# A two-layer backbone on one core: other places, queues and order around the FFN stage

## The chip, the cores and the metric

The kernel runs on one core of one Trainium2 chip. The metric is the device time of one execution in microseconds (us); the kernel before took 3029.22 us, the median of three runs. PE is TensorE, DVE VectorE, ACT ScalarE, POOL GpSimd. SP is the engine that only issues transfers here. PE, DVE, ACT, POOL and SP each run their own list of instructions in order, and a list is written ahead of time by a planner that goes by its own estimates of durations.

## The reference

Two layers of one trunk, float32 throughout, for 1024 latent tokens and 256 context tokens of width 1024:

```python
for l in range(DEPTH):                       # DEPTH = 2
    need_ctx = l < DEPTH - 1                 # the context leaves after layer 0's keys, values and FFN
    mod_l = split(silu(c) @ mod_w[l] + mod_b[l], 6); mod_c = the same of c_ctx
    h_lat, h_ctx = modulate(rmsnorm(x_lat), ...), modulate(rmsnorm(x_ctx), ...)
    y_lat, y_ctx = hybrid_mixer(h_lat, h_ctx, ...)      # GLA, gMLP and windowed attention, one w_in, one w_out
    x_lat = x_lat + mod_l[2] * rmsnorm(y_lat)
    f_lat = swiglu(modulate(rmsnorm(x_lat), mod_l[3], mod_l[4]), w_gu[l], w_down[l])
    x_lat = x_lat + mod_l[5] * rmsnorm(f_lat)
    if need_ctx: the same two steps for x_ctx with mod_c
def swiglu(h, w_gu, w_down):
    g, u = split(h @ w_gu, 2)                # D_FF = 2816: 22 chunks of 128
    return (silu(g) * u) @ w_down
```

## The kernel before

**Products.** Each float32 product is made of three products of high and low parts (`mm3`, L307). `halve` makes the parts: a cast on ACT (L1404) and a difference on DVE (L1405).

**Layer.** `layer` (L1170) runs projection; GLA (`gla_stream`) and windowed attention (`swa_stream`) merged; `mix_out`; the up stage (`Up.stream`); in layer 0 alone `up_context`; and `down_stage`. Each stage has pools of SBUF, opened and closed on the left or right side, and a pool may lie over one that has closed. The planner orders by whole pools; the waits that it then sets are by tile.

**mix_out (L1250).** The concatenated row tiles `cat` come back from DRAM (`xt`, L1274), are turned on PE (L1269), and meet w_out (L1289), whose rows are loaded by `weight` (L1261) through two staging tiles rg and ru that belong to the up stage. `ao` (GLA, L955) and `co` (attention, L1077) are stored to `cat` by SP, the last `co` of a layer by POOL. `post` and `norm` of a tile give the FFN's input; parts of it (s3, s4, a22) go through DRAM and come back by two buffers `hc` in `waiting` (L1386).

**Up stage.** For each of 22 chunks, seven half-size products of 12 matmuls of 512 columns stand for eight. In order: X = b11·a11, copy p1 (L201, ACT); Y = b21·a12, add g0 (L204, DVE) and its Silu (ACT); X += t2·s2, copy u2 (L211, ACT); Z = t1·s1, copy p5 (L214, ACT); X += t3·s3, add c22 (L223, DVE); Z += b22·s4, add c12 (L230, DVE); X += t4·a22, Silu. Differences of weights for the next chunk are on POOL (L174), results go to DRAM `gd` from POOL.

**Context pass (L1408).** The context's 256 tokens, 22 chunks of 48 matmuls; ch and cl are the halves of its input, loaded by two `hc` (L1427), gh, gl, uh, ul those of the weights.

**Down stage (L1445).** Token halves of five tiles (layer 1: four), each in groups of chunks (`sizes`); a group holds its weights (`weight`, ws, L1456) and activations (`acts`, g), does its products (L1111) and adds into ya (L1118); the last group's tiles go through `post`.

**Background modulation.** While layer 0 runs its FFN, DVE computes seven vectors of modulation that come later: `mod_stream("dve")`, seven pieces of 16 steps, each step a load of 256 KB (ms, L421) and two multiply-adds (macc, L503 and L505); a fold on PE (L447) and transposes (L455) end a piece. `paced` advances it by a step each time the planned costs that the stage yields sum to MOD_STEP = 6.6.

## Time and profile before

| | before |
|---|---|
| median of 3 runs | 3029.22 us (3026.78 to 3031.38) |
| profiled execution | 3032.15 us, span 3030.4 us |
| PE busy | 2802.9 us (92%) |
| DVE busy | 1905.1 us (63%) |
| ACT busy | 1333.0 us (44%) |
| POOL busy | 691.8 us (23%) |
| read and written, over the span | 121 GB/s |

The page gives shares over the whole span, and a share is an average over stages with different limits. So it is read for the engine that carries the chain, and then the trace is asked stage by stage: busy times in a table by stretches, the waits of an engine with what ended them, and the timeline of an engine for one border. Layer 0's w_out begins near 617 us, its up stage near 765, the context pass near 1246, the down stage near 1397; layer 1's w_out near 2190, its up stage near 2318 and its down stage near 2769.

### The profile page before, as it was taken

The page shows a single profiled execution, that of the slowest core. Times are in us where ns is not written, and L with a number is a line of the kernel's source. Part 1 is how long each engine was busy: PE and PEld are TensorE (multiplying, and loading weights), DVE is VectorE, ACT ScalarE, POOL GpSimd, SP SyncE. Part 2 cuts the span into 40 slices and gives each one's busy share as a digit, 9 for nine tenths or more (in the row PEclk, how much of TensorE's full clock was granted, in tenths as well). Part 3 has the DMA queues.
Part 4 walks back from the last instruction along what each step waited for, and adds up shares of the span by engine and source line. Part 5 has one row for each costly group of instructions (what it writes and reads, how often), then busy time and mean ns, then how long its engine had stood idle before and what let it go on. Part 6 is the DMA issues. An engine that isn't in the chain of part 4 may idle for free.

```text
span 3030.4 us, 43735 instructions
## 1 busy us (share of the span) xinstructions
PE 2802.9 (92%) x16296; PEld 2383.9 (79%) x16296; DVE 1905.1 (63%) x3663; ACT 1333.0 (44%) x2739; POOL 691.8 (23%) x562
## 2 busy tenths in 40 slices
PE   6999899989799999897999999999896999999998
PEld 4999788867677778796788899888775788887886
DVE  3565577866947874377578665788757434344576
ACT  4453576745433233343233245477545333334331
POOL 0000233301454445100000000043302455552000
PEclk8999799999899999998999999999998999999999
DMA  7843000055533442586365354200254222224452
GB/s 233 254 141 89 24 12 9 31 199 180 181 96 106 140 131 83 163 253 211 109 208 163 97 148 117 70 8 11 69 190 153 79 77 81 84 81 168 154 195 90
DMA packets 337809, 370.45 MB, mean 122 GB/s; under 512 B 45296, under 2 KB 259068, under 8 KB 337596
## 3 DMA queue, kind: packets, MB, share of 16 engines
q1 hardware_dynamic: 327244, 335.93, 36.0%
q0 software_dynamic: 9632, 29.11, 2.6%
q8 instruction: 128, 2.10, 0.3%
q10 hardware_dynamic: 720, 2.62, 0.2%
q14 instruction: 85, 0.70, 0.1%
HBM read 300.19 MB, written 67.40 MB: 121 GB/s over the span
## 4 chain that ended last, share of the span: by engine, by line
PE 67%; DVE 13%; DMA 9%; ACT 5%; issue 4%; POOL 1%; SPq 1%; DVEq 0%; ACTq 0%; POOLq 0%
PE b L307 35%; PE b L1111 17%; DMA ms<-in_mod_w 3%; PE b L1012 2%; PE b L1030 2%; PE b L1047 2%; DVE macc L505 2%; PE b L1289 2%; PE b L896 1%; DMA ru<-in_w_out 1%; PE b L884 1%; DMA ws<-in_ffn_w_down 1%; ACT hc L1333 1%; DVE pe L1017 1%; DVE z L1311 1%
## 5 line engine op out<-in xcount | busy, mean ns | idle before, releaser
L1111 PE MATMUL b<-dh,g 128*128 128x512 f32 x828 | 229.5, 396 | 22.1 <-ACT dh L1404 18.6
L1111 PE MATMUL b<-wh,g 128*128 128x512 f32 x756 | 210.3, 396 | 1.7 <-DVE ya L1118 1.7
L1111 PEld LDWEIGHTS b<-dh,g 128*128 128x128 f32 x828 | 157.5, 191 | 57.4 <-ACT dh L1404 19.0
L1118 DVE TENSOR_TENSOR ya<-ya,b 128x512 f32<-128x512 f32 x198 | 127.6, 683 | 109.0 <-PE b L1111 108.9
L505 DVE SCALAR_TENSOR_TENSOR macc<-ms,csil,macc 128x512 f32<-128x512 f32 x196 | 171.0, 907 | 32.7 <-DMA ms<-in_mod_w 31.4
L307 PE MATMUL b<-wh,hh 128*128 128x256 f32 (+1 forms) x592 | 173.2, 294 | 8.6 <-DVE hh L540 3.8
L307 PE MATMUL b<-wh,hl 128*128 128x256 f32 (+1 forms) x592 | 171.4, 290 | 1.2 <-DVE hl L541 1.2
L307 PE MATMUL b<-wl,hh 128*128 128x256 f32 (+1 forms) x592 | 171.8, 290 | 0.4 <-DVE wl L614 0.3
L1111 PEld LDWEIGHTS b<-wh,g 128*128 128x128 f32 x756 | 141.8, 188 | 36.2 <-DVE ya L1118 2.2
L614 DVE TENSOR_TENSOR wl<-ws,wh 128x1024 fp32r<-128x1024 f32 (+2 forms) x68 | 79.7, 1177 | 130.1 <-ACT wh L613 130.0
L307 PE MATMUL b<-hh,wh 128*128 128x320 f32 (+1 forms) x472 | 148.8, 315 | 0.0
L307 PE MATMUL b<-hl,wh 128*128 128x320 f32 (+1 forms) x472 | 147.2, 312 | 0.0
L307 PE MATMUL b<-hh,wl 128*128 128x320 f32 (+1 forms) x472 | 146.9, 311 | 0.0
L1111 PE MATMUL b<-dl,g 128*128 128x512 f32 x414 | 130.0, 395 | 0.1
L1036 DVE TENSOR_TENSOR ptl<-b,pth 128x640 fp32r<-128x640 f32 (+2 forms) x144 | 107.5, 746 | 33.9 <-ACT pth L1035 32.6
L613 ACT CAST wh<-ws 128x1024 fp32r<-128x1024 f32 (+2 forms) x68 | 68.8, 1014 | 136.0 <-PE b L307 80.3
L1035 ACT CAST pth<-b 128x640 fp32r<-128x640 f32 (+2 forms) x144 | 91.0, 632 | 75.6 <-PE b L1030 74.6
L307 PEld LDWEIGHTS b<-wh,hh 128*128 128x128 f32 x592 | 114.4, 193 | 12.5 <-issue 5.5
L231 POOL TENSOR_TENSOR ct<-ct,ct 128x512 f32<-128x512 f32 x44 | 71.8, 1631 | 212.8 <-DVE ct L230 184.5
L1111 PE MATMUL b<-wl,g 128*128 128x512 f32 x378 | 119.0, 395 | 0.0
L1017 DVE CUSTOM_DVE_ANT_0 pe<-b,swm,sink 128x640 f32<-128x640 f32 (+1 forms) x128 | 108.1, 845 | 13.8 <-PE b L1012 13.1
L307 PEld LDWEIGHTS b<-wh,hl 128*128 128x128 f32 x592 | 114.4, 193 | 1.6 <-DVE hl L541 1.6
(380 smaller groups left out, 8544.2 us busy)
## 6 DMA issues: line engine op xcount, KB each, us to landing
ws<-in_ffn_w_down SPq DMA_DIRECT2D x88, 512.0 KB, 3.6
ms<-in_mod_w SPq DMA_DIRECT2D x144, 256.0 KB, 3.5
rg<-in_ffn_w_gu SPq DMA_DIRECT2D x66, 512.0 KB, 3.8
ru<-in_ffn_w_gu SPq DMA_DIRECT2D x66, 512.0 KB, 3.9
ws<-in_w_in SPq DMA_DIRECT2D x56, 512.0 KB, 4.4
gd<-ct POOLq DMA_DIRECT2D x88, 256.0 KB, 2.9
gr<-gd SPq DMA_DIRECT2D x44, 320.0 KB, 3.6
gr<-gd SPq DMA_DIRECT2D x44, 256.0 KB, 3.6
```

What stands on the lines that cost most here:

```text
L231: nc.gpsimd.tensor_mul(g0, g0, c12)
L307: mm = lambda x, y, **kw: self.nc.tensor.matmul(out, x, y, skip_group_check=more, **kw)
L505: nc.vector.scalar_tensor_tensor(x, st, c, x, op0=ALU.mult, op1=ALU.add)
L613: nc.scalar.copy(h[:, : kk * nn], st[:, : kk * nn])
L614: nc.vector.tensor_sub(lo[:, : kk * nn], st[:, : kk * nn], h[:, : kk * nn].bitcast(F32))
L1012: nc.tensor.matmul(ps[:, at : at + n * P], b["qs"][:, h, :], kk[:, j * P : (j + n) * P], start=(n_ == 0), stop=(n_ == 1))
L1017: nc.vector.tensor_tensor_reduce(out=p, in0=sc, in1=b["mask"], scale=1.0, scalar=sink, op0=ALU.add, op1=ALU.min, accum_out=mn)
L1030: nc.tensor.transpose(pt[:, j * P : (j + 1) * P], p[:, j * P : (j + 1) * P], self.ident)
L1035: nc.scalar.copy(hi, pv)
L1036: nc.vector.tensor_sub(lo, pv, hi.bitcast(F32))
L1111: nc.tensor.matmul(ps[n], x[:, s], y[:, n * 512 : (n + 1) * 512], start=(c == 0 and pi == 0), stop=(c == nk - 1 and pi == 2))
L1118: nc.vector.tensor_add(y, y, ps[n])
```

## The change

Six things change. (1) rg and ru get a pool of their own (rp, right side), w_out's halves and GLA's tiles are laid out in another order, and all stores of `ao` and `co` go by POOL. (2) `Up.stream` does the first two products of chunks 0 and 1 ahead of everything else, each chunk is cut into `head` and `tail`, and the Silu of g0 stands behind the copies u2 and p5. (3) In layer 0 the last tile's `post` and `norm` come behind these heads; in layer 1 its `post` has a higher priority; the last tile's transposes use one double bank. (4) The modulation starts behind chunk 1, has a step of 5.4 in the up stage and 6.6 in the down stage, none in the context pass; a gate's transposes are put off to a later step. (5) The context pass takes the place of the up stage's first operands (fa), and loads hc ahead of its weights. (6) The down stage lies on the right, its first weights in wp, its activations where the context pass had its input; the second half has six groups instead of seven.

```diff
+        self.head(0)
+        self.prepare(1, "b11")
+        self.prepare(1, "b21")
+        self.head(1)
+        yield 0.0
         for c in range(NFC):
-            yield from self.chunk(c)
+            if c > 1:
+                self.head(c)
+                yield 5.4
+            yield from self.tail(c)
...
         nc.scalar.copy(p5, Z)
-        if more:
+        net.act(g0, g0, AF.Silu)
+        if 1 < n < NFC:
             self.prepare(n, "b11")
             self.prepare(n, "b21")
+        if more:
             self.diff(n, "t1")
...
             if gate:
-                to_rows(ps)
+                self.later = lambda: to_rows(self.b1())
...
-            nc.sync.dma_start(self.cat[i][:, 0:256], ao)
+            nc.gpsimd.dma_start(self.cat[i][:, 0:256], ao)
...
-            (nc.gpsimd if i == blocks[-1] else nc.sync).dma_start(self.cat[i][:, 512:1024], co)
+            nc.gpsimd.dma_start(self.cat[i][:, 512:1024], co)
...
-            self.paced(st)
-            up.close()
+            with tp("rp", "right") as rp:
+                up = Up(self, l, fa, rp, A)
...
+                    next(st)
+                    if need_ctx:
+                        next(rest)
+                        for _ in range(8):
+                            next(st)
+                    for _ in rest:
+                        pass
...
+                self.paced(st, 5.4)
+                up.close()
         if need_ctx:
-            with tp("cu", "right") as cu:
-                self.paced(self.up_context(l, cu, up))
+            with tp("cu", "left") as cu:
+                self.up_context(l, cu, up)
         self.open_hp()
-        with tp("dn", "left") as dn:
-            self.paced(self.down_stage(l, dn, need_ctx, up.gd))
+        with tp("dn", "right") as dn:
+            self.paced(self.down_stage(l, dn, need_ctx, up.gd), 6.6)
...
-        W = [(self.t(wo, f"oh{k}", [P, D], F32R), self.t(wo, f"ol{k}", [P, D], F32R)) for k in range(KC)]
+        W = {}
+        for k in (7, 6, 0, 1, 2, 3, 4, 5):
+            if k == 0:
+                for x in ("ch", "cl"):
+                    self.t(wo, x, [P, KC, P], F32R, bufs=2)
+            W[k] = self.t(wo, f"oh{k}", [P, D], F32R), self.t(wo, f"ol{k}", [P, D], F32R)
...
+        up.load(1)
         waiting(slice(0, 256))
         if need_ctx:
             waiting(slice(256, 512))
+            yield
+            post(order[-1])
+            yield
+            norm(order[-1])
+            return
         yield
-        post(order[-1])
-        if not need_ctx:
-            waiting(slice(256, 384))
+        with self.tc.high_priority(offset=250):
+            post(order[-1])
+        waiting(slice(256, 384))
         norm(order[-1])
...
-            pool, tags = ((dn, ("dl", "dh")), (self.wp, ("wl", "wh")))[loads[0] % 2]
+            pool, tags = ((self.wp, ("wl", "wh")), (dn, ("dl", "dh")))[loads[0] % 2]
...
-        sizes = [[2, 4, 4, 4, 4, 4], [4, 3, 3, 3, 3, 3, 3]]
+        n = len(halves[0]) * P
+        self.t(dn, "g", [P, 2, n], F32R, bufs=8), self.t(dn, "gr", [P, n], bufs=2)
+        sizes = [[2, 4, 4, 4, 4, 4], [4, 4, 4, 4, 4, 2]]
```

## Rows read from the trace of the kernel before

**Rows 1.** The page's part 4: the chain that ended last, share by engine.

```profile
PE 67%; DVE 13%; DMA 9%; ACT 5%; issue 4%; POOL 1%; SPq 1%; DVEq 0%; ACTq 0%; POOLq 0%
```

**Rows 2.** Stages: stretch, length, PE PEld DVE ACT POOL busy (x count), clock, DMA.

```profile
880.00:940.00 60.00, 60.00 (x269) 48.76 (x268) 25.52 (x37) 21.50 (x37) 30.37 (x25) 1.00 0.27 84
940.00:1040.00 100.00, 87.97 (x350) 69.08 (x349) 95.65 (x114) 27.82 (x50) 40.23 (x33) 0.93 0.50 145
1257.00:1397.00 140.00, 132.57 (x1065) 131.26 (x1065) 98.90 (x128) 55.81 (x74) 10.96 (x21) 0.96 0.86 248
2374.00:2769.00 395.00, 395.00 (x1716) 322.70 (x1714) 153.80 (x200) 137.53 (x238) 198.29 (x159) 1.00 0.25 79
```

**Rows 3.** Waits of PE, 813 to 1246 us: awaited: total us, times, longest.

```profile
PE b L307 <- ACT ct L211: 22.1, 8, 3.6
```

**Rows 4.** Timeline of PE at layer 0's w_out: start, us, instruction, idle before.

```profile
626.12 1.22 PE L1289 MATMUL b<-oh,ch 128*128 128x512 f32 x2 [8.99 <-ACT ch L1279]
```

**Rows 5.** Waits of PE, 755 to 840 us.

```profile
PE b L1269 <- DVE ht L1315: 9.5, 1, 9.5
PE b L307 <- ACT ct L211: 5.8, 2, 3.6
```

**Rows 6.** Timeline of PE, layer 1's end of mix_out.

```profile
2336.13 1.94 PE L1269 MATMUL b<-ident,ht 128*128 128x128 f32 x8 [11.81 <-DVE ht L1315]
```

**Rows 7.** Waits of PE, 1257 to 1397 us, the context pass.

```profile
PE b L307 <- ACT ch L1404: 10.9, 1, 10.9
PE b L455 <- DVE gate L465: 4.7, 1, 4.7
```

**Rows 8.** Waits: PE, 1397 to 1760 us; SP, 1390 to 1415 us.

```profile
PE b L1111 <- ACT dh L1404: 18.6, 2, 15.4
SPq L421 <- DVE macc L505: 13.2, 8, 2.6
```

**Rows 9.** Timeline of SP ahead of layer 0's w_out.

```profile
613.40 0.87 SPq L951 DMA_DIRECT2D gld<-gsp  x2
616.60 0.32 SPq L955 DMA_DIRECT2D cat<-ao  x1
616.97 0.42 SPq L1261 DMA_DIRECT2D rg<-in_w_out  x1
```

**Rows 10.** Busy time by stage, the end of layer 0's attention.

```profile
545.00:617.00 72.00, 66.81 (x574) 58.67 (x572) 67.06 (x189) 50.06 (x135) 32.43 (x36) 0.98 0.19 61
```

**Rows 11.** Timeline of POOL, the last store of co in layer 0.

```profile
620.29 0.61 POOL L1077 DMA_DIRECT2D cat<-co  x1 [2.56 <-DVE co L1075]
```

**Rows 12.** The page's part 6: transfer, queue, count, KB each, median us to landing.

```profile
gd<-ct POOLq DMA_DIRECT2D x88, 256.0 KB, 2.9
cat<-co SPq DMA_DIRECT2D x16, 256.0 KB, 2.0
```

**Rows 13.** Busy time of the instructions on macc, 940 to 1040 us.

```profile
940.00:1040.00 100.00, 67.40 (x70) 0.93 0.50 145
```

**Rows 14.** Timelines of PE and DVE: the wait for L211 and the add L223.

```profile
980.49 0.50 PE L307 MATMUL b<-s3h,t3h 128*128 128x512 f32 x1 [2.83 <-ACT ct L211]
987.22 0.68 DVE L223 TENSOR_TENSOR ct<-b,ct 128x512 f32<-128x512 f32 x1
```

**Rows 15.** Timeline of SP ahead of the context pass.

```profile
1248.47 4.60 SPq L1427 DMA_DIRECT2D hc<-hd  x2
```

**Rows 16.** The page's part 5: a cast and a difference of 128 by 1024.

```profile
L614 DVE TENSOR_TENSOR wl<-ws,wh 128x1024 fp32r<-128x1024 f32 (+2 forms) x68 | 79.7, 1177 | 130.1 <-ACT wh L613 130.0
L613 ACT CAST wh<-ws 128x1024 fp32r<-128x1024 f32 (+2 forms) x68 | 68.8, 1014 | 136.0 <-PE b L307 80.3
```

**Rows 17.** Timeline of SP ahead of the down stage.

```profile
1406.88 0.90 SPq L1456 DMA_DIRECT2D ws<-in_ffn_w_down  x2
```

**Rows 18.** Busy time by stage, the kernel's end.

```profile
3004.80:3030.40 25.60, 12.44 (x55) 9.95 (x54) 21.39 (x64) 4.61 (x8) 0.00 (x0) 0.85 0.36 124
```

**Rows 19.** Waits of SP, 2130 to 2240 us.

```profile
SPq L1077 <- DVE co L1075: 47.8, 2, 27.0
```

More of the change, by code (lines that the diff above doesn't have):

```diff
@@ L29 @@
 GLA_SHARE = (105.0, 83.0)
-MOD_SHARE_PROJ, MOD_STEP = 100.0, 6.6
+MOD_SHARE_PROJ = 100.0
 MOD_LATE = 3
@@ L189, in stream, with head @@
     def stream(self):
-        for c in range(NFC):
-            yield from self.chunk(c)
-    def chunk(self, c):
-        nc, net, n = self.nc, self.net, c + 1
-        more = n < NFC
-        X, Y, Z = net.b1(), net.b1(), net.b2()[:, :512]
-        store = lambda at, t: nc.gpsimd.dma_start(self.gd[c][:, at : at + 512], t)
+        self.head(0)
[3 more added lines that the diff above has]
+        yield 0.0
+        for c in range(NFC):
+            if c > 1:
+                self.head(c)
+                yield 5.4
+            yield from self.tail(c)
+    def head(self, c):
+        nc, net = self.nc, self.net
+        X, Y = net.b1(), net.b1()
         self.product(X, c, "b11", "a11", True)
@@ L204, in chunk, with tail @@
         nc.vector.tensor_add(g0, Y, p1)
-        net.act(g0, g0, AF.Silu)
-        yield 5.4
-        if more:
+        self.begun[c] = X, g0
+    def tail(self, c):
+        nc, net, n = self.nc, self.net, c + 1
+        more = n < NFC
+        X, g0 = self.begun.pop(c)
+        Z = net.b2()[:, :512]
+        store = lambda at, t: nc.gpsimd.dma_start(self.gd[c][:, at : at + 512], t)
+        if 1 < n < NFC:
             self.load(n)
@@ L379, in mod_stream @@
             yield from self.mod_piece(way, l, j)
-        self.mod_rest()
-        yield 1.0
-        self.mod_rest()
+        for _ in range(3):
+            self.mod_rest()
+            yield 1.0
     def mod_rest(self):
-        for f in (self.later, self.late):
-            if f:
-                self.later = None
-                f()
-        self.late = None
+        f, self.later = self.later, None
+        if f:
+            f()
+        f, self.late = self.late, None
+        if f:
+            f()
     def mod_piece(self, way, l, j):
@@ L1217, in layer, with paced @@
             A = {x + p: self.t(fa, x + p, [P, 4, 512], F32R) for x in ("a11", "a12", "s2", "s1") for p in "hl"}
-            up = Up(self, l, fa, A)
-            with tp("px", "left") as px:
-                rest = self.mix_out(l, px, A, up, tp)
-                next(rest)
-                st = up.stream()
-                next(st)
-                for _ in rest:
-                    pass
-            if l + 1 < self.layers:
-                self.mring = self.fix, 2
-                self.back = self.mod_stream("dve", [(0, 5)] + [(l + 1, j) for j in (1, 0, 2, 3, 4, 5)])
-            self.paced(st)
-            up.close()
+            with tp("rp", "right") as rp:
+                up = Up(self, l, fa, rp, A)
+                with tp("px", "left") as px:
+                    rest = self.mix_out(l, px, A, up, tp)
+                    next(rest)
+                    st = up.stream()
+                    next(st)
+                    if need_ctx:
+                        next(rest)
+                        for _ in range(8):
+                            next(st)
+                    for _ in rest:
+                        pass
+                if l + 1 < self.layers:
+                    self.mring = self.fix, 2
+                    self.back = self.mod_stream("dve", [(0, 5)] + [(l + 1, j) for j in (1, 0, 2, 3, 4, 5)])
+                self.paced(st, 5.4)
+                up.close()
         if need_ctx:
-            with tp("cu", "right") as cu:
-                self.paced(self.up_context(l, cu, up))
+            with tp("cu", "left") as cu:
+                self.up_context(l, cu, up)
         self.open_hp()
-        with tp("dn", "left") as dn:
-            self.paced(self.down_stage(l, dn, need_ctx, up.gd))
+        with tp("dn", "right") as dn:
+            self.paced(self.down_stage(l, dn, need_ctx, up.gd), 6.6)
         for _ in self.back:
             pass
-    def paced(self, stream):
+    def paced(self, stream, step):
         for cost in stream:
             self.spent += cost
-            while self.spent >= MOD_STEP:
-                self.spent -= MOD_STEP
+            while self.spent >= step:
+                self.spent -= step
                 next(self.back, None)
@@ L1262, in weight, with turn @@
             self.halve(*W[k], t)
-        def turn(src, f):
+        def turn(src, f, wide=False):
+            both = self.b2() if wide else None
             for q in range(2):
-                ps = self.b1()
+                ps = both[:, q * 512 : q * 512 + 512] if wide else self.b1()
                 for k in range(4):
@@ L1335, in part @@
                         nc.vector.tensor_scalar(to, pv[:, k, :], scale, shift, op0=ALU.mult, op1=ALU.add)
-            turn(zs.pop(i), part)
+            turn(zs.pop(i), part, i == order[-1])
             split = lambda x, v: self.halve(A[x + "h"][:, :, s], A[x + "l"][:, :, s], v)
@@ L1422, in load @@
                 have[-1].append(w)
-        load(0)
         for i in range(CT):
@@ L1429, in up_context @@
             self.halve(ch[:, :, s], cl[:, :, s], t)
+        load(0)
         for c in range(NFC):
@@ L1540, in gla_consts @@
         nc, a = self.nc, self.a
+        for tag, shape, dt, bufs in (("ei", [4, P], F32, 2), ("ep", [1024], F32, 1), ("ds", [TT, P], F32, 1), ("lv0", [4, P], F32, 2),
+                                     ("lv1", [4, P], F32, 2), ("osq", [256], F32, 1), ("gld", [256], F32, 2), ("ao", [256], F32, 2)):
+            x = self.t(gp, tag, [P] + shape, dt, bufs=bufs)
+            if tag == "ds":
+                self.ds = x
         self.gml = self.t(gp, "gml", [P, 256], U8)
```

18 lines of the change are left out of this document (9 added, 9 removed).

## The prediction

> **What bounds the kernel now.** I read the page's chain first. PE carries 67% of it; the rest is DVE, DMA and ACT, so what can be won is the time in which PE waits or runs slowly, stage by stage [rows 1]. Then the table by stages: layer 1's up stage, without background modulation, runs 1716 products in 395 us. Layer 0's up stage does the same work, but its stretch 940 to 1040 us holds 350 products where a calm stretch of 60 us holds 269, and DVE is busy for 95.65 of those 100 us [rows 2]. PE's waits in that stage are 22.1 us for the copy at L211 and next to nothing else [rows 3]. Last, the waits at the borders between stages, where PE stands still because the next stage's first operand isn't there: 8.99 us ahead of the w_out product, and as long a wait once more in layer 1 [rows 4], 9.5 and 11.81 us ahead of the last tile's transposes [rows 5, 6], 10.9 us ahead of the context pass [rows 7], 15.4 us ahead of the down stage [rows 8]. These borders sum to some 66 us, 2.2% of the span, and the change works on each.
>
> **w_out, both layers (staging in a place of its own, cat stores on POOL).** SP issues in order. The first w_out load (616.97 us) leaves right behind the store of ao (616.60 us), which had waited for POOL; the gld loads ahead of both are issued by 613.40 + 0.87 = 614.3 us [rows 9]. Layer 1 repeats this pattern. With the stores on POOL the load can start at 614.3, 2.7 us earlier, and with cast and difference behind it unchanged PE gains as much: 2 x 2.7, rounded to +6, for some of the xt loads come earlier too. Upper bound +12: two gaps of 9 us less 3 us each for the transposes and the cast of ch that still come. Lower bound 0: the list that the planner writes keeps the load behind something as late. The stores cost POOL 0.61 us of issue each, as the one that it has already [rows 11]; 34 move (16 of co, 18 of ao), 17 a layer, some 10 us, and POOL is busy for 32.43 of 72 us at the end of layer 0's attention, so they fit [rows 10]. Behind a waiting store on POOL stand the multiplications L938 and L954; PE's product L940 and the ao stores wait for these. That is the third rival.
>
> A store of 256 KB lands 2.0 us after its issue on SP and 2.9 us on POOL [rows 12]; the last one of each layer can stand in the chain, at most 2 x 0.9 us, which the rounding of the bounds holds. The Trainium skill ("SBUF — State Buffer", section "SBUF: two separate sides") speaks against this part: descriptors of a transfer issued from GpSimd are written by GpSimd, which a VectorE operation that holds the shared port locks out; it gives some 620 ns alone and 3100 ns beside such an operation. By that, two last stores would cost an estimated 5 us, and this part of the sum would be +1. The trace has 88 stores of gd beside a busy DVE at 2.9 us in the median, so I go by the row.
>
> **End of mix_out and layer 0's up stage.** Two heads (products b11·a11 and b21·a12 of chunks 0 and 1) now come ahead of chunk 0's tail, and the last tile's post and norm behind them. The 9.5 us [rows 5] is time in which PE had nothing ready; a head is 24 products, 5.4 us at 60/269 us each [rows 2], and two of them cover the gap. Of the 5.8 us for L211 in this stretch [rows 5], which hang on loads of hc through two buffers that the change leaves alone, I count a quarter: +11. Against it stands DVE. A step of the modulation is two multiply-adds. The stream now starts at chunk 2 with a step for each 5.4 of planned cost: 20 chunks x 18.9 / 5.4 = 70 steps in the stage, where it had 22 x 18.9 / 6.6, 62. In 940 to 1040 us, 70 multiply-adds [rows 13] cost 100 - 350 x 60/269 = 21.9 us, 0.31 us each; sixteen more cost 5 us. Net +6. Upper bound +10: all of 9.5 and 5.8, less 5. Lower bound -10: half of the 9.5, and the 32 multiply-adds of the first burst, which ran at the end of mix_out while PE stood, now under products: 48 x 0.31 = 15.
>
> **Silu behind the copies.** In before, the Silu of g0 waits for DVE's add L204, and the copy L211 stands behind it on ACT, so PE waits. Moving it can take away up to 22.1 us [rows 3]. I take 0, nearer to the end at which the wait only moves: DVE is full in these stretches [rows 2], and the product t4·a22 waits for DVE's add L223 on the same X. Around 980 us PE waits 2.83 us for L211, starts at 980.49, and runs 24 products until the add L223 at 987.22 [rows 14] lets it go on at once; 2.8 us earlier it would have met that add instead.
>
> **Layer 1's end of mix_out.** The gap is 11.81 us [rows 6]. The trace has chunk 1's head ahead of chunk 0's tail there already, and the binding loads are those of hc; the higher priority of the last post brings it forward by a few DVE operations. +2 (0 to 8).
>
> **Context pass.** The first product waits 10.9 us for ch [rows 7]. The hc loads are issued from 1248.47 us on, after the last product of the up stage, and SP is through with them 4.60 us later [rows 15]. In the new place ch lies over a11h, hc over a12, gh over s2l: the last chunk's head reads a11 and a12 for the last time, and six and five products of 2.7 us follow, four and three after s2 and s1. So 8 us at the least are free for loads (4.6 us by that row), a cast and a difference (1.0 and 1.2 us [rows 16]), if the queues' order allows. I leave 2 us of gap: +9 (5 to 11). Within the pass the fold's wait of 4.7 us (gate, L465) [rows 7] goes with the modulation, which has no steps here now, and the granted clock is 0.96 over its 140 us [rows 2], worth 5.6 us, of which I count 2 as owed to the standstills: +7 (4 to 10).
>
> **Context pass to down stage.** The first weight ws is issued at 1406.88 us [rows 17], after SP waited 13.2 us for multiply-adds to free the modulation's buffers [rows 8]; transfer and cast follow. The place of the first weights (wp, and the right side) is now free during the context pass, so they can arrive before it ends. The first slots of g lie over ch and cl and wait for the last context product; what is left is a cast and a difference, 1.0 + 1.2 us [rows 16], and 1 us for queues: 15.4 - 3.2 = +12 (8 to 14). In the down stage the modulation gets 43 steps where it had 34: 18 multiply-adds at 0.31 us are 5.6 us, but with 34 steps that stage's other wait for a weight is only 18.6 - 15.4 = 3.2 us [rows 8], so I take -2 (-8 to 0).
>
> **Tails.** The second half's groups are 4,4,4,4,4,2 chunks instead of 4,3,3,3,3,3,3. A tile takes 18 products in a last group of three and 12 in one of two, 4.1 and 2.8 us at 395/1716 [rows 2]. DVE finishes a tile in 5.3 us (21.39 us busy for four tiles [rows 18]) and is the bound once the first tile is through: with two chunks it starts 4 x 1.4 = 5.5 us later against the end of PE, less some of the adds of the group that is saved. In layer 0 the next layer's norms come one behind each group but the first, so with six groups the fifth moves behind the last one; the lower end holds that. -4 in layer 0 (-7 to 0) and -4 at the kernel's end (-5 to -2).
>
> **Sum.** +6 +6 +0 +2 +9 +7 +12 -2 -4 -4 = +32 us. The profiled execution took 3032.15 us (span 3030.4), 2.93 above the median of 3029.22. 3032.15 - 32 - 2.93 = **2997 us**.
>
> **The rivals.** First: the up stage stays bound by DVE and pays for every step; DVE's 95.65% [rows 2] speaks for it, the calm stretch beside it against it, since an even spread of the steps would fit. The stage gives -10 in the place of +6: 3013 us. Second: the change doesn't do what it says. If the planner orders the queues by whole places, the context pass's loads and the down stage's weights still stand behind the old users; +9 and +12 are lost: 3018 us. Third, the slower side: a co store on POOL waits for DVE, and what is queued behind it waits as well. On SP such waits were 47.8 us in two pieces in layer 1 alone [rows 19]. If POOL stood so long, GLA's products would come late by as much: 48 us lost, and the +6 of w_out, so 3051 us. It decides from 32 us of such standing on. Against it speaks that SP could wait because nothing else was queued, while the planner writes POOL's list with the store where it expects co. Fourth: more is won. If w_out's loads go ahead of the gld loads, the gaps fall by 6 us more, and if three quarters of L211's 22.1 us return, 17: 2974 us.
>
> **How the numbers follow.** Forecast's case 0.57, first rival 0.2, second 0.08, third 0.05, fourth 0.1. A measurement of this kernel tells about 0.2%, 6 us, from no change, so a time under 3023 is faster: the forecast, the first, the fourth and most of the second. The third is slower. With the bounds' ends counted in, same has 0.06 and slower 0.06, which leaves 0.88. The range reaches from a little below the fourth rival, 2966, to a little above the second, 3022, and leaves out the third and the far ends.
>
> **What would show it.** Right: PE's wait ahead of the context pass under 3 us and ahead of the down stage under 5; gaps of 6 us at w_out; no fold in the context pass, and its length near 130 us; no 9 us gap at the last tile's transposes in layer 0. The first rival shows as waits for L223 or L1405 in layer 0's up stage with DVE over 90%; the second as hc or ws loads issued after the last product of the stage before; the third as POOL idle for DVE co at L1077 with PE waiting for L938. What would make the sum wrong is above all the 0.31 us for a multiply-add: if the bursts fall apart, the up stage is worth 20 us more.

## The result and the profile after

The changed kernel took 2994.65 us, the median of four runs (2990.82 to 3000.45), against 3029.91 us before: a ratio of 0.9887 (95% interval 0.9869 to 0.9905). The forecast was 2997 us. The profiled execution has a span of 2992.7 us where the one before had 3030.4. One slow execution, of the run with the last group of four, took 3983.66 us at a granted clock of 0.645, and the median given for that run is of its other three.

Line numbers have moved. Of those named here: mm3 is L321, the copy u2 is L223 (before L211), the add c22 L237 (L223), the g0 add L210, every Silu L295, casts and differences of `halve` L1437 and L1438, w_out's loads L1286, xt loads L1300, the down products L1125, the fold L462, multiply-adds L518 and L520.

The first table gives the stretches between the first or last product of each kind on PE's timeline, beside the terms of the sum (a gain is negative; the profile models the end of a product, so a stretch can come out just below 0).

| stretch, us | before | after | change | term |
|---|---|---|---|---|
| start to the first score product | 345.7 | 343.4 | -2.3 | 0 |
| from there to the first w_out product, layers 0 and 1 | 280.5 + 229.9 | 281.5 + 234.2 | +5.3 | -6 |
| w_out to the end of the up stage, layer 0 | 620.3 | 612.6 | -7.7 | -6 |
| up stage to context pass | 10.9 | -0.2 | -11.1 | -9 |
| context pass | 139.3 | 128.3 | -11.0 | -7 |
| context pass to down stage | 15.4 | 4.4 | -11.0 | -12 |
| layer 0's down stage to layer 1's first score product | 558.3 | 562.4 | +4.1 | +6 |
| layer 1: w_out to the end of the up stage | 568.7 | 565.4 | -3.3 | -2 |
| layer 1: end of the up stage to the end | 261.3 | 260.6 | -0.7 | +4 |
| sum | | | -37.7 | -32 |

The start takes 342 to 347 us in all the kernels of this study, with the same code, so the first row is no effect. Layer 1 has to be read over two rows: from its first score product to the end of its up stage the kernel before takes 798.6 us, the changed one 799.6, and all the kernels of this study 796.3 to 802.5. What it loses up to w_out it wins behind it. PE turns two row tiles of `cat` ahead of the first w_out product there, where it turned one; the busy time of these transposes (L1269, now L1295; columns PE, PEld, clock, DMA) in the stretch, before and after:

```profile
1970.40:2200.30 229.90, 3.88 (x16) 3.14 (x16) 0.96 0.11 34
```

```profile
1932.50:2166.70 234.20, 7.76 (x32) 6.28 (x32) 0.95 0.12 39
```

So 3.9 of the 4.3 us that this stretch grew by are work that was done earlier.

Table by stages of the changed kernel (columns as in [rows 2]):

```profile
860.00:960.00 100.00, 100.00 (x444) 81.60 (x443) 41.30 (x55) 35.75 (x62) 52.97 (x43) 1.00 0.28 86
960.00:1120.00 160.00, 142.59 (x574) 112.98 (x573) 151.84 (x185) 45.14 (x81) 67.78 (x53) 0.93 0.49 140
1238.00:1366.00 128.00, 126.73 (x1054) 126.52 (x1054) 63.65 (x67) 52.10 (x67) 13.86 (x24) 1.00 0.71 212
2341.00:2732.00 391.00, 390.96 (x1704) 319.62 (x1704) 154.63 (x200) 136.26 (x236) 198.14 (x158) 1.00 0.25 80
```

The calm stretch, the burst of multiply-adds and the clean stage of layer 1 look as in [rows 2]: 574 products in the 160 us of the burst where a calm stretch of 100 us holds 444, and DVE busy for 151.84 of them. The context pass is what is new: PE is busy for 126.73 of its 128 us, at a granted clock of 1.00 where it was 0.96.

Waits of PE in layer 0's up stage, to be read beside [rows 3]:

```profile
PE b L321 <- ACT ct L223: 24.1, 8, 5.2
PE b L321 <- DVE ct L237: 0.5, 2, 0.4
```

The same eight waits, for the same copy. The instructions on macc, in the up stage of the kernel before, then in the up stage and the context pass of the changed one:

```profile
760.00:1246.00 486.00, 133.80 (x144) 0.95 0.39 116
```

```profile
760.00:1237.00 477.00, 135.73 (x144) 0.96 0.41 124
1237.00:1366.00 129.00, 0.00 (x0) 1.00 0.71 211
```

Waits of PE in the context pass and from the down stage to the next projection (for [rows 7, 8]):

```profile
PE b L321 <- DVE gl L1438: 1.2, 1, 1.2
```

```profile
PE b L1125 <- ACT g L1437: 4.4, 1, 4.4
...
PE b L462 <- DVE modr L454: 13.9, 1, 13.9
```

The two borders are gone but for 4.4 us, and a wait of 13.9 us for a fold is new. At layer 0's w_out, SP's timeline, PE's row and SP's waits (for [rows 9, 4]):

```profile
613.74 3.39 SPq L1300 DMA_DIRECT2D xt<-cat  x2
617.18 1.61 SPq L1286 DMA_DIRECT2D rg<-in_w_out  x1
```

```profile
624.99 1.22 PE L1315 MATMUL b<-oh,ch 128*128 128x512 f32 x2 [8.21 <-ACT ch L1305]
```

```profile
SPq L1300 <- PE b L1295: 3.9, 2, 2.6
...
SPq L1286 <- DVE rt_b L358: 1.7, 1, 1.7
```

The store is no longer ahead of the load, but an xt load is, which waits for PE's transposes; the load leaves SP no earlier than before, and then waits 1.7 us more for an operation of DVE. PE's gap is 8.21 us where it was 8.99, so the 6 us that were to show there did not come.

### The profile page after: what moved, and what is told of

Read it like the earlier page. It is cut to its first block, busy times and chain, and to the rows that moved or that the text cites. A ratio compares the mean times of both kernels' runs of the same rounds, so it can differ in the third digit from the quotient of the medians.

```text
span 2992.7 us, 43649 instructions
## 1 busy us (share of the span) xinstructions
PE 2793.8 (93%) x16296; PEld 2379.0 (79%) x16296; DVE 1900.3 (63%) x3645; ACT 1329.3 (44%) x2739; POOL 712.4 (24%) x596
## 5 line engine op out<-in xcount | busy, mean ns | idle before, releaser
L1125 PE MATMUL b<-wh,g 128*128 128x512 f32 x792 | 218.6, 393 | 8.6 <-ACT g L1437 7.9
L1125 PE MATMUL b<-dh,g 128*128 128x512 f32 x792 | 215.4, 390 | 2.0 <-DVE ya L1132 0.9
L520 DVE SCALAR_TENSOR_TENSOR macc<-ms,csil,macc 128x512 f32<-128x512 f32 x196 | 178.8, 945 | 20.6 <-DMA ms<-in_mod_w 19.9
L1125 PEld LDWEIGHTS b<-wh,g 128*128 128x128 f32 x792 | 149.1, 189 | 43.4 <-ACT g L1437 8.9
L321 PE MATMUL b<-wh,hh 128*128 128x256 f32 (+1 forms) x592 | 173.5, 294 | 5.1 <-DVE hh L555 3.8
L1125 PEld LDWEIGHTS b<-dh,g 128*128 128x128 f32 x792 | 148.5, 188 | 34.8 <-DVE ya L1132 3.4
L321 PE MATMUL b<-wh,hl 128*128 128x256 f32 (+1 forms) x592 | 171.4, 290 | 1.3 <-DVE hl L556 1.2
L1132 DVE TENSOR_TENSOR ya<-ya,b 128x512 f32<-128x512 f32 x180 | 115.9, 681 | 88.2 <-PE b L1125 88.1
L321 PE MATMUL b<-wl,hh 128*128 128x256 f32 (+1 forms) x592 | 171.7, 290 | 0.0
L321 PE MATMUL b<-hh,wh 128*128 128x320 f32 (+1 forms) x472 | 148.9, 315 | 0.0
L321 PE MATMUL b<-hl,wh 128*128 128x320 f32 (+1 forms) x472 | 147.2, 312 | 0.0
L321 PE MATMUL b<-hh,wl 128*128 128x320 f32 (+1 forms) x472 | 146.9, 311 | 0.0
L1125 PE MATMUL b<-wl,g 128*128 128x512 f32 x396 | 123.5, 392 | 0.4 <-DVE wl L1438 0.4
L1125 PE MATMUL b<-dl,g 128*128 128x512 f32 x396 | 122.3, 389 | 0.0
L321 PEld LDWEIGHTS b<-wh,hh 128*128 128x128 f32 x592 | 114.5, 194 | 8.9 <-issue 4.7
L321 PEld LDWEIGHTS b<-wh,hl 128*128 128x128 f32 x592 | 114.6, 194 | 1.9 <-DVE hl L556 1.9
```

Source lines behind the costliest of these rows:

```text
L321: mm = lambda x, y, **kw: self.nc.tensor.matmul(out, x, y, skip_group_check=more, **kw)
L520: nc.vector.scalar_tensor_tensor(x, st, c, x, op0=ALU.mult, op1=ALU.add)
L1125: nc.tensor.matmul(ps[n], x[:, s], y[:, n * 512 : (n + 1) * 512], start=(c == 0 and pi == 0), stop=(c == nk - 1 and pi == 2))
L1132: nc.vector.tensor_add(y, y, ps[n])
```

## The experiments

All but one start from the changed kernel. Stretches in us, from one profile of each kernel; the last column is the ratio to the kernel before with its 95% interval. The kernel before was timed again beside each group of runs, with medians of 3029.91 to 3035.37, so kernels compare by their ratios better than by their medians.

| run | to w_out, layers 0, 1 | up stage 0 | to the pass | pass | to down | down 0 to scores 1 | tail | median us | ratio |
|---|---|---|---|---|---|---|---|---|---|
| changed kernel | 281.5, 234.2 | 476.0 | -0.2 | 128.3 | 4.4 | 562.4 | 15.0 | 2994.65 | 0.9887 [0.9869, 0.9905] |
| stores on SP | 280.7, 235.8 | 476.7 | -0.2 | 128.3 | 4.4 | 562.0 | 15.0 | 2993.54 | 0.987 [0.9849, 0.9891] |
| step 6.0 | 280.7, 233.5 | 476.6 | -0.2 | 128.3 | 4.4 | 565.6 | 15.9 | 3001.38 | 0.9898 [0.9881, 0.9915] |
| Silu last | 282.3, 232.3 | 476.8 | -0.2 | 128.3 | 4.4 | 561.2 | 15.0 | 2993.74 | 0.9875 [0.9856, 0.9894] |
| modulation in the pass | 282.9, 233.6 | 478.3 | -0.2 | 133.9 | 14.1 | 567.8 | 14.8 | 3020.56 | 0.9958 [0.9941, 0.9974] |
| places back | 282.6, 235.0 | 477.5 | 5.7 | 133.2 | 2.8 | 561.8 | 14.9 | 3009.89 | 0.9929 [0.9911, 0.9946] |
| one head | 281.9, 234.6 | 478.8 | -0.2 | 128.4 | 4.4 | 563.2 | 15.0 | 2999.57 | 0.989 [0.9875, 0.9906] |
| norm early, step 6.0 | 274.1, 233.6 | 477.5 | -0.2 | 128.3 | 4.4 | 563.3 | 14.8 | 2994.51 | 0.9877 [0.9856, 0.9898] |
| last group of four | 281.6, 234.1 | 479.0 | -0.2 | 128.3 | 4.4 | 560.8 | 11.0 | 2993.81 | 0.9855 [0.9822, 0.9888] |
| spread | 281.9, 232.2 | 437.0 | -0.2 | 133.1 | 4.4 | 562.8 | 14.8 | 2958.44 | 0.9757 [0.9738, 0.9775] |
| kernel before, spread | 279.3, 231.6 | 441.2 | 16.2 | 145.9 | 14.3 | 557.0 | 13.1 | 2997.09 | 0.9882 [0.9851, 0.9912] |
| spread, last group of four, norm early, step 6.0 | 281.8, 233.3 | 437.0 | -0.2 | 132.5 | 4.4 | 548.9 | 11.0 | 2945.42 | 0.9706 [0.9681, 0.9731] |
| the same, first w_out loads on ACT | 284.0, 225.6 | 437.0 | -0.2 | 132.5 | 4.4 | 550.3 | 12.1 | 2947.54 | 0.9718 [0.9701, 0.9734] |

### The stores back on SP

```diff
-            nc.gpsimd.dma_start(self.cat[i][:, 0:256], ao)
+            nc.sync.dma_start(self.cat[i][:, 0:256], ao)
...
-            nc.gpsimd.dma_start(self.cat[i][:, 512:1024], co)
+            (nc.gpsimd if i == blocks[-1] else nc.sync).dma_start(self.cat[i][:, 512:1024], co)
```

> The changed kernel with the stores of ao and co back on SP (the last co of a layer on POOL, as in the kernel before); everything else as changed. Stages of the changed kernel, first score product of the attention to first w_out product: 281.6 us in layer 0, 234.3 in layer 1 (before: 280.4 and 229.9). Theory: the stores on POOL cost, since each stands between two multiplications of ao and lands later, and the w_out load gained nothing by the move because an xt load took the place of the store ahead of it on SP. Then layer 1 falls back to about 230, layer 0 stays within 1.5 us of 281, and the whole is 3 to 5 us faster than the changed kernel. Rival: the new layout and order of the tiles cost it, not the queue: both numbers stay as in the changed kernel. Second rival: the move does gain, hidden by something else: both rise by 3 or more.

Measured: 280.7 and 235.8. Layer 1 did not fall back, so the theory is wrong and the first rival holds: the queue of these stores gains nothing and costs nothing that can be told here. Layer 1's stretch is 232.2 to 235.8 us in all the kernels with the changed layout and SP's w_out loads, 229.9 and 231.6 in the two with the old one; most of that is the row tile that PE turns earlier (table of stretches), and it comes back by the end of the up stage. In layer 0 the profiles of one and the same code spread from 274.1 to 282.9, and nothing smaller can be told.

### A step for each 6.0 in the down stage

```diff
-            self.paced(self.down_stage(l, dn, need_ctx, up.gd), 6.6)
+            self.paced(self.down_stage(l, dn, need_ctx, up.gd), 6.0)
```

> The changed kernel with one number other: the modulation has a step for each 6.0 of planned cost in the down stage, not 6.6, so that all 115 steps lie inside the stages (70 + 47) and not 113. The changed kernel has a new wait of 13.9 us of PE at 1686 us, for a fold whose sums had been ready since about 1650 us: its finish stands behind the posts in DVE's list. Theory: the two steps left over are written behind the whole down stage, so the fold comes late; with them inside, the wait goes, and the time falls by 8 to 14 us (some steps more at 0.3 us each). Rival: DVE's posts bound this tail anyway; PE then waits for the next layer's operands in its place, and less than 5 us is gained.

The fold came at 1658.6 us and its wait went, but PE's waits in the stretch show what took its place, longer than the one removed:

```profile
PE b L321 <- DVE hh L555: 17.4, 1, 17.4
```

hh is the next projection's operand, made from the fifth of the next layer's norms. In the changed kernel DVE's timeline shows the same queue from the other side: the sums of the fold are taken up behind the posts' adds (L1159), 49 us behind the last multiply-add at 1647.9.

```profile
1696.18 1.22 DVE L1159 TENSOR_TENSOR ya<-ya,xp 128x1024 f32<-128x1024 f32 x1
1697.31 1.30 DVE L453 STREAM_TRANSPOSE ht<-macc 128x512 f32<-128x512 f32 x2
1698.64 1.22 DVE L454 TENSOR_REDUCE modr<-ht 128x32 f32<-128x1024 f32 x1
```

So the wait is a matter of what stands behind the posts, and either operand will do. This was the rival; the whole was no faster (0.9898 against 0.9887).

### The Silu behind the copies, by an order

```diff
-        nc.scalar.copy(p5, Z)
-        net.act(g0, g0, AF.Silu)
+        cp = nc.scalar.copy(p5, Z)
+        net.order(net.act(g0, g0, AF.Silu), cp)
```

> The changed kernel with an order added: the Silu of g0 stands behind the copy p5 in ACT's list. In the changed kernel's list the planner had put it ahead of the copy u2 all the same, as in the kernel before, so the edit of the change did nothing, and PE still waits 24.1 us for that copy (L223). Theory (DVE is the bound in the bursts): the 24 us of waits for the copy go, but 15 us or more of them come back as waits for the add c22 (L237) or for halves; layer 0's up stage stays at 476 us within 6. Rival: the copy was the bound; the stage falls to 452 to 460 us and the time by 15 to 24 us.

ACT's timeline of the changed kernel: the Silu of g0 still runs ahead of the copy L223, and had waited for DVE's add; the planner had undone the edit.

```profile
986.80 0.63 ACT L295 ACTIVATE ct<-ct 128x512 f32<-128x512 f32 x1 [6.04 <-DVE ct L210]
987.34 0.60 ACT L1437 CAST t2h<-tt 128x512 fp32r<-128x512 f32 x1
987.84 0.58 ACT L223 COPY ct<-b 128x512 f32<-128x512 f32 x1
```

With the order forced, PE's waits in the stage are:

```profile
PE b L321 <- DVE ct L237: 28.5, 8, 6.2
...
PE b L321 <- ACT ct L223: 0.2, 1, 0.2
```

28.5 us for the add where 24.1 were for the copy, and the stage at 476.8 us. The theory holds: the wait moves from the copy to the add, so in the bursts DVE is the bound.

### The modulation in the context pass again

```diff
-                self.up_context(l, cu, up)
+                self.paced(self.up_context(l, cu, up), 6.6)
...
             nc.gpsimd.dma_start(up.gd[c][:, 0:256], g)
+            yield 5.8
```

> The changed kernel with the modulation advanced in the context pass again, a step for each 6.6 of planned cost, 5.8 a chunk; places, queues and order as changed. It parts what the place gave from what the modulation's absence gave. Theory: the place gives the start (10.8 us before, none now) and the absence gives the pass (139.4 us before, 128.3 now): then the start stays under 2 us and the pass returns to 134 to 139. The wait ahead of the down stage (15.3 before, 4.4 now) stays under 6 if the place is its cause, and returns to 10 or more if SP's loads for the modulation, queued ahead of the weights, were. The late fold at 1686 us goes, since the steps end earlier. Sum: within 5 us of the changed kernel. Rival: the pass stays at 128 with the modulation in it; then its gain was the place's too.

The start stayed at -0.2, the pass returned to 133.9, half of the way to the 139.3 before, and the wait ahead of the down stage to 14.1 us. The waits of PE and, below, of SP:

```profile
PE b L1125 <- ACT g L1437: 14.2, 1, 14.2
PE b L321 <- DVE gl L1438: 4.0, 4, 1.2
...
SPq L436 <- DVE macc L520: 11.5, 7, 2.4
```

SP stands behind its own loads for the modulation (L436), as in [rows 8], and the first operands of the down stage come late by that, although their place is free. The sum was not within 5 us: in the tail PE waits 16.9 us for hh where it had waited for the fold, and the run's profile is 24 us longer.

### The places put back

```diff
-            with tp("cu", "left") as cu:
+            with tp("cu", "right") as cu:
...
-        with tp("dn", "right") as dn:
+        with tp("dn", "left") as dn:
...
-            pool, tags = ((self.wp, ("wl", "wh")), (dn, ("dl", "dh")))[loads[0] % 2]
+            pool, tags = ((dn, ("dl", "dh")), (self.wp, ("wl", "wh")))[loads[0] % 2]
```

> The changed kernel with the places of the context pass and the down stage put back: the pass on the right over the up stage's second half, the down stage on the left with its first weights there; order, queues and modulation (none in the pass) as changed. Together with the run that put the modulation back it parts place from modulation. Theory: the place alone opens the pass early, so PE's wait between the up stage and the pass returns from 0 to 9 to 12 us; the wait ahead of the down stage, which the modulation's loads caused, stays under 8, since SP has nothing else queued; the pass stays at 128 us. Sum 10 to 15 us slower than the changed kernel, about 3007. Rival: the place carries both borders, and the wait ahead of the down stage returns to 13 to 16 as well: about 3017.

```profile
PE b L321 <- ACT gh L1437: 6.3, 2, 5.7
PE b L1125 <- ACT dh L1437: 2.8, 1, 2.8
```

The theory was right on the down stage alone: the wait ahead of it did not come back (2.8). The one ahead of the pass came back by half, 5.7 us and not 9 to 12, and the pass took 133.2 us and not 128. So the place is worth 6 us of the first border and 5 of the pass; the second border is owed to the modulation's absence. That no modulation load stands ahead of the hc loads may be the other half of the first; this run doesn't tell it from the new order of those loads.

### One head ahead instead of two

```diff
-        self.head(0)
-        self.prepare(1, "b11")
-        self.prepare(1, "b21")
-        self.head(1)
-        yield 0.0
         for c in range(NFC):
-            if c > 1:
-                self.head(c)
-                yield 5.4
+            self.head(c)
+            yield 5.4
             yield from self.tail(c)
...
```

(the loads, preparations and steps that hang on the second head move with it)

> The changed kernel with one thing undone in the up stage: each chunk's first two products come right ahead of its own rest, not two chunks begun ahead; the last tile's post and norm in layer 0 still come behind the rests of chunks 0 and 1. Stages of the changed kernel: layer 0's up stage 476.0 us (before 483.5), layer 1's w_out to the end of the up stage 565.4 (before 568.7). Theory: the two heads cover the wait of the last tile's norm, so layer 0's up stage rises by 3 to 8 us to 479 to 484, and layer 1 by 1 to 4. Rival: the later place of post and norm did it alone; then layer 0 stays within 2 us of 476 and only layer 1 moves.

478.8 us in layer 0, and 565.8 from layer 1's w_out to the end of its up stage. The kernels above and below that have both heads and the same up stage, not spread, take 476.0 to 479.0 us there, and the ratio is 0.989 against 0.9887: nothing that the second head is worth can be told. Neither run has the 9.5 us wait of [rows 5], so that wait went with the later place of post and norm, which both runs have, and not with the second head.

### The multiply-adds spread

```diff
-        nc.vector.tensor_add(g0, Y, p1)
+        net.anchor = nc.vector.tensor_add(g0, Y, p1)
...
-                        nc.vector.scalar_tensor_tensor(x, st, c, x, op0=ALU.mult, op1=ALU.add)
+                        r = nc.vector.scalar_tensor_tensor(x, st, c, x, op0=ALU.mult, op1=ALU.add)
+                    if self.anchor:
+                        self.order(r, self.anchor)
```

(the adds c22 and c12 are anchors too, and the first multiply-add of a sum is ordered in the same way)

> The changed kernel with an order added for the modulation's multiply-adds: each stands in DVE's list behind the up stage's add that was written last when it was written, so the planner can't gather them ahead in bursts; in the up stage there are then 7 or so in each chunk. The work is the same. It tests the 0.31 us a multiply-add. Theory: the price is one of bursts, when DVE has more than 20 us of work for a chunk's 19.4; spread, DVE has 8.5 + 7 x 1.0, some 16 us a chunk, and the waits for the copy and the add (24.6 us in the changed kernel) fall under 6; layer 0's up stage goes from 476 to 450 to 460 us. Rival: each multiply-add costs by itself, since it shares its port with POOL's differences (0.74 us alone, up to 2 us beside them); then the stage stays at 470 or above.

437.0 us, below the theory's range. From 820 to 1180 us, the engines and the instructions on macc; then all that PE waited for from 800 us to the end of the stage:

```profile
820.00:1180.00 360.00, 360.00 (x1591) 293.75 (x1590) 287.93 (x350) 128.35 (x223) 186.61 (x148) 1.00 0.43 127
```

```profile
820.00:1180.00 360.00, 138.84 (x145) 1.00 0.43 127
```

```profile
PE b L321 <- DVE ct L237: 1.6, 1, 1.6
```

145 instructions on macc in 360 us, DVE busy for 288 of them, and PE runs 1591 products without a wait at a granted clock of 1.00. So spread multiply-adds cost PE nothing; a burst of them does. The context pass behind the stage took 133.1 us where it had 128.3, with 3.6 us of waits for cl and gl at its start and a granted clock of 0.97; why they come back there stays open. With it the spread gains some 34 us.

The same order in the kernel before:

> The kernel before with the order of the spread run alone: the multiply-adds of the modulation stand behind the up stage's last written add in DVE's list. Theory: the 0.31 us a multiply-add was the price of bursts in the kernel before as well; its layer 0 up stage falls from 483.5 us to 455 to 465 us, the rest stays, and the time is about 3006. The changed kernel with the spread took 437.0 us there and 2958 us; the difference of the two is what the rest of the change is worth without bursts, some 45 us. Rival: without the two heads the stage keeps its waits at the end of mix_out and for the copy behind the Silu; it stays at 470 or above.

441.2 us in the up stage and 2997.09 us in all, below the theory's figures for both, so the theory holds and its size was too small: the order alone is worth as much in the kernel before (0.9882) as the whole change (0.9887). The two add up, 0.9757. The border and the context pass of this run took 16.2 + 145.9 us; more of the modulation fell into them, 74 instructions on macc where there had been 50.

### The tails

```diff
-        sizes = [[2, 4, 4, 4, 4, 4], [4, 4, 4, 4, 4, 2]]
+        sizes = [[2, 4, 4, 4, 4, 4], [2, 4, 4, 4, 4, 4]]
```

> The changed kernel with the second half's groups of chunks in the other order, 2,4,4,4,4,4: still six, but the last has four chunks. It tests the price of the tails. Theory: what ends a layer is DVE's and ACT's posts (some 5.3 to 7 us a tile), which begin when the last group's first tile is through; with four chunks PE has 5.5 us a tile beside them. Then the stretch from the down stage's first product to layer 1's first score product, 562.4 us in the changed kernel and 558.3 before, falls to 550 to 557; the kernel's tail behind the last product falls from 15.0 to 9 to 11 us; the time falls by 9 to 16 us, to about 2982. Rival: in layer 0 the late fold and the fifth norm set the end, whatever the group's size: 560 to 563 there, and only 4 to 6 us are gained at the kernel's end.

The tail at the kernel's end fell to 11.0 us as expected. In layer 0 the rival holds, 560.8: the fold's wait shrank to 1.8, but PE waits for the small first group's copies on ACT, whose places the first half's results still hold. The median, 2993.81, doesn't show the 4 us of the end; the ratio, 0.9855, may, but its interval reaches to 0.9888.

```profile
PE b L1125 <- ACT ya L1130: 8.9, 2, 6.6
PE b L462 <- DVE modr L454: 1.8, 1, 1.8
PE b L470 <- DVE rs_y L335: 1.6, 1, 1.6
```

The fifth norm ahead of the last group, with steps of 6.0:

```diff
-            if hi == 1 and cs.start and nxt:
+            if hi == 1 and nxt:
                 nxt.pop(0)()
-                if len(nxt) == 1:
+                if not nxt:
```

> The changed kernel with a modulation step for each 6.0 in the down stage and the next layer's norms written one behind each of the second half's first five groups, the first of them included, so that the fifth is ahead of the last group as in the kernel before. The run with 6.0 alone put the fold at 1659 us and PE then waited 17.4 us for hh of the fifth norm, which DVE does behind the posts. Theory: the stretch from the last product of the down stage to layer 1's first score product, 236.9 us before and 250.9 in the changed kernel, comes back to 236 to 240, and the time falls by 10 to 13 us, to about 2983. Rival: DVE's posts hold some third operand of the projection too; then less than half of it is gained.

563.3 us: fold and hh are in time, and PE waits for a third thing.

```profile
PE b L321 <- ACT code L687: 10.8, 1, 10.8
```

This was the rival: the stretch gained nothing. All of it together, with the spread:

> The changed kernel with four edits: the multiply-adds spread, the second half's groups 2,4,4,4,4,4, the fifth norm ahead of the last group, and a step for each 6.0 in the down stage. Theory: the up stage keeps its 437 us, the layer 0 tail no longer waits for the fold or the fifth norm (562.4 us from the down stage's first product to layer 1's first score product falls to 548 to 555), the kernel's tail falls to 9 to 11 us: about 2944, 14 below the spread alone. Rival: the tails are bound by the posts with any grouping; then it is within 6 us of the spread alone, 2952 to 2958.

```profile
PE b L1127 <- ACT ya L1132: 4.6, 2, 3.0
PE b L321 <- ACT code L689: 0.6, 1, 0.6
```

548.9 us in layer 0, 11.0 at the end, 2945.42 us: the fastest kernel of the study. Each edit of the tail alone gave at most 1.6 us in layer 0; together, with the spread, which alone gave nothing there (562.8), they gave 13.5 us, since one operand after another stood behind the posts.

### w_out's first loads on ACT

```diff
-            nc.sync.dma_start(t, a["w_out"][l, k * P : (k + 1) * P, :])
+            (nc.scalar if k < 2 else nc.sync).dma_start(t, a["w_out"][l, k * P : (k + 1) * P, :])
```

> The kernel of the last run (changed kernel, spread, groups 2,4,4,4,4,4, fifth norm early, steps of 6.0) with the first two loads of w_out of each layer issued by ACT instead of SP. In layer 0 they left SP at 617.5 us, right behind the second xt load, which had waited for PE; the first w_out product came at 625.6, in layer 1 281.8 and 233.3 us are the stretches from first score product to first w_out product. Theory: the planner orders by whole pools, so in ACT's list too the loads stand behind the last operations of the attention's pools; they leave at 617 us or later, and both stretches stay within 2 us. Rival: SP's queue is what holds them; then they leave near 614, the two stretches fall by 3 to 4 us each, and the time is near 2938.

ACT's timeline in layer 0, with an end of the attention's norm right ahead of the load:

```profile
618.45 0.20 ACT L295 ACTIVATE rt_y<-rt_y 128x1 f32<-128x1 f32 x1
618.51 0.34 ACTq L1288 DMA_DIRECT2D rg<-in_w_out  x1
```

In layer 0 the theory holds: another queue, and the load stands behind the attention's last operations in that list as well, 284.0 us. In layer 1 the stretch fell by 7.7 us, as the rival has it and by more; but the time from w_out's last product to the up stage rose from 3.2 to 10.1 us there, which is what the kernel before has. From the first score product to the end of the up stage layer 1 took 798.1 us where it had 799.3, and the whole is unchanged (0.9718 against 0.9706).

## Why the prediction was right, and where not

**The time** was right within 2.4 us, and that closeness is in part luck. By the profiles one term, w_out, was off by 11.3 us to the bad, and all others together, the start included, by 17.0 to the good. Three terms lie outside their own ranges to the good (the start of the context pass and the pass by little, the kernel's end by 2.7 us), and one, w_out, to the bad.

**w_out** (+6) failed: the two stretches lost 5.3 us, of which layer 1's 4.3 come back behind it, so the term was worth about nothing. The step that failed is "with the stores on POOL the load can start at 614.3". The rows of SP after show the next thing in the queue, the second xt load, leaving at the same time as the store had; the bound of 0 was named for this. In layer 1 PE waits for xt, then for rt_b and for oh, where before it waited for xt (7.3 us) and for ch (9.4):

```profile
PE b L1295 <- DMA xt<-cat: 6.1, 3, 3.0
PE b L1295 <- DVE rt_b L358: 5.5, 1, 5.5
PE b L1315 <- ACT oh L1437: 4.5, 1, 4.5
```

These waits are no longer than before in sum, so the stretch grew by the tile turned earlier and not by them. The stores themselves landed in 2.3 us (co) and 2.9 us (ao), where SP's took 2.0 (co) [rows 12] and 1.9 (ao):

```profile
cat<-co POOLq DMA_DIRECT2D x18, 256.0 KB, 2.3
...
cat<-ao POOLq DMA_DIRECT2D x18, 128.0 KB, 2.9
```

The Trainium skill ("SBUF — State Buffer", section "SBUF: two separate sides") gives some 3100 ns, where 620 would do, for a transfer issued from GpSimd beside a VectorE operation that holds the shared port. The trace has 0.3 us more for co and 1.0 for ao, and the run with the stores on SP has the same time, so the rule's case did not decide anything here. The third rival did not come either: at the end of layer 0's attention POOL stood for co for 3.7 us in two pieces, where 32 us would have decided.

```profile
POOL cat L1091 <- DVE co L1090: 3.7, 2, 2.8
```

**The up stage** (+6) gave 7.7 and was right in size, but in part for other reasons. It credits two heads with covering the gap; the run with one head shows that the later post and norm did it. Its count was wrong: the planner puts 144 instructions on macc in the stage in both kernels, whatever the step, so no sixteen were added; and the 70 of [rows 13] are 62 multiply-adds and 8 transposes that close a sum. The price of 0.31 us was a mean over a burst, as "what would make the sum wrong" says; spread, it is nothing, and the stage won 39 us and not the 20 named there. So the first rival had the bound right: in the bursts it was DVE, and an even spread did fit. **Silu** (0) was right, and for the reason given, but what was measured there in the changed kernel was no edit at all, since the planner undid it; only the forced order shows the reason.

**Layer 1's end of mix_out** (+2) gave 3.3 by its row, but together with the stretch ahead of it nothing (table of stretches). The 11.81 us gap [rows 6] is gone; PE waits for the weights of chunk 1's head in its place, which the step does not name:

```profile
PE b L321 <- ACT b11h L1437: 9.6, 1, 9.6
```

**The context pass**: the start (+9) gave 11.1, by the step named: SP issues the hc loads at 1223.39 us, 14 us ahead of the first product, and half of the gain needs the place (the run with the places back):

```profile
1223.39 0.81 SPq L1461 DMA_DIRECT2D hc<-hd  x2
```

The pass (+7) gave 11.0, just over its range of 4 to 10, as all of the lost clock came back and not 2 us of it. The step credits the modulation's absence alone; the runs give it 5.6 us, and 4.9 us to the place, which the step does not name. Most of the lost clock lay right behind the 10.9 us standstill ahead of the pass, at 0.50 (1.2 GHz) over its first 7.3 us in the kernel before:

```profile
1257.40:1264.70 7.30, 6.62 (x29) 6.33 (x30) 3.58 (x3) 3.10 (x3) 0.00 (x0) 0.50 1.20 290
```

**To the down stage** (+12) gave 11.0, but the step credits the place; the runs show that the modulation's loads on SP were the cause and that the old place does as well once they are gone.

**Down stage and tail of layer 0** (-6 together) gave -4.1, from larger parts: the stage itself shortened by 9.9 us and the stretch behind it grew by 14.0. Some 20 of PE's operations moved from the one into the other, and the end of the stage ran at full clock, as the table by stages shows for the kernel before and, below it, the changed one:

```profile
1706.00:1733.50 27.50, 24.32 (x99) 19.75 (x98) 21.28 (x50) 10.82 (x18) 0.00 (x0) 0.88 0.54 170
```

```profile
1660.00:1681.60 21.60, 20.84 (x97) 16.95 (x96) 16.77 (x40) 7.87 (x14) 0.00 (x0) 1.00 0.37 99
```

What was not seen is that 70 + 43 steps are two short of the stream's 115, so that the last fold stands behind the posts. **Layer 1's tail** (-4) gave +0.7. The step's 5.5 us for posts that start later was too much: the time behind the last product rose from 13.1 to 15.0 us, and the stage ahead of it shortened by 2.6. That the saved adds did this is not shown; that the last group's size sets the end is, by the 11.0 us with a group of four.

## What to carry to other kernels

Work that is to fill an engine's idle time costs nothing when it is spread and a great deal when a planner gathers it: here the same multiply-adds cost 39 us of one stage in bursts and none there when each was tied to a step of the foreground. An edit in a source that a planner reorders has to be looked for in the engine's list before its effect is priced. Where a tail's operands stand one behind another in an in-order list, mending one shows the next; count all of them before the first is mended.

## What the runs showed of the hardware

With DVE at 288 of 360 us busy and POOL at 187 of them, PE kept its full rate and a granted clock of 1.00 for 360 us; in the burst the clock was 0.93 with 17 us of standstills in 160, and its 574 products took 142.59 us, 0.248 each where calm ones take 0.225, 13 us in all. The 0.93 is a mean of two levels. The burst has six standstills of PE, of 2.5 to 3.2 us, and by each of them the granted clock falls to 0.50 (1.2 GHz) for 3.4 or 6.8 us and rises to 1.00 (2.4 GHz) again; the first of them on PE's timeline, and the stretch by stages right behind it:

```profile
988.47 0.50 PE L321 MATMUL b<-s3h,t3h 128*128 128x512 f32 x1 [2.54 <-ACT ct L223]
```

```profile
989.10:992.50 3.40, 3.40 (x10) 2.63 (x9) 3.40 (x7) 0.33 (x1) 0.00 (x0) 0.50 0.10 11
```

The spread kernel has neither a standstill nor a stretch at 1.2 GHz in its 360 us. Of the 39 us that the spread won in the stage, 23 are waits that went, and the other 16 are, as far as these rows tell, products that run at 2.4 GHz again. No run here changes the clock without the standstills; that the standstills bring it down is read from where the falls lie.
